# The last block's input products one group ahead, output operands three row tiles ahead, and the next stage's weights behind the residuals

## The chip, the cores and the metric

The kernel runs on one core of a Trainium2 chip. The metric is the device time of one execution in microseconds (us). A core has five engines with queues of their own: PE (TensorE: matrix products, and transposes done as products), DVE (VectorE), ACT (ScalarE), POOL (GpSimd) and SP (SyncE, which here issues nearly all DMAs). Each engine takes its instructions in the order written; between engines they wait on semaphores.

## The reference

One inference step of a small hybrid decoder: a recurrent layer (Hawk/Griffin RG-LRU), then a layer of forgetting attention. It runs on a prompt of 2048 new tokens and on 8 sequences of 8 new tokens each, which have 4096 tokens behind them in a paged cache. The width is 1024, 16 heads of 64. All is in float32.

```python
def recurrent_mixer(x, h0, conv_buf, w_in, conv_w, conv_b, w_ga, b_ga, w_gx, b_gx, lam, w_out):
    z = x @ w_in
    u, g = z[..., :D_RNN], z[..., D_RNN:]
    u, new_buf = causal_conv(u, conv_buf, conv_w, conv_b)
    h, h_last = rg_lru(u, h0, w_ga, b_ga, w_gx, b_gx, lam)
    return (h * jax.nn.silu(g)) @ w_out, h_last, new_buf

# in rg_lru, over 8 blocks of 128 columns:
    r = sigmoid(ub @ w_ga + b_ga); i = sigmoid(ub @ w_gx + b_gx)
    log_a = -RGLRU_C * r * softplus(-lam); a = exp(log_a)
    h[t] = a * h[t-1] + sqrt(-expm1(2 * log_a)) * (i * u)

# in run_group: layer 0 is recurrent, then the shared keys and values, then attention
x = x + rms_norm(recurrent_mixer(rms_norm(x, a_pre_norm), ...), a_post_norm)
k, v, logf = shared_kv(x, kv_norm, w_kv, b_f)
x = x + rms_norm(fox_mixer(rms_norm(x, b_pre_norm), k, v, ...), b_post_norm)
```

The outputs are both x, the new keys, values and log forget values, and the recurrent and convolution states.

## The kernel before

The tokens are worked in two chunks. Chunk 0 has the 64 sample tokens (all 8 sequences) and 1024 prompt tokens, chunk 1 the rest. A float32 product is made of three products of rounded parts (`mm3`): high by high (L367), low by high (L368), high by low (L369). So a float32 operand exists as two tiles, such as `uh` and `ul`.

**Recurrence** (`phase_a1`). For each of 8 column blocks (`KB` = 8, index `n`), the chunk's tokens come in three groups (320, 384 and 384 columns in chunk 0; 384, 384 and 256 in chunk 1). For a group, PE makes the u columns (24 matmuls), ACT copies them out of PSUM (`up`), DVE does the convolution (`uc`), POOL rounds it to `uh`, DVE makes the rest `ul`. Then come the gate products (6 matmuls, `gate`) on `uh` and `ul`, and PE makes the g columns (24 matmuls). The gates of one group are issued after the u product of the next one, ahead of its g product (`pend`, `gated`). ACT turns gates into decay, DVE scans the recurrence, POOL multiplies by the gated g (`tg`), and the result, as `oh` and `ol`, is written to DRAM by SP (L641, L642).

**Output** (`phase_a2`). For each row tile of up to 128 tokens, SP loads the transposed operands `ohT` and `olT` back (L757) and the residual rows `xt` (L759). PE makes the product with w_out in two halves of 512 columns (`y`, 24 matmuls each) in the order (0,0), (1,0), (0,1), (1,1), (2,0), (2,1) and so on, first the tile and then the half. PSUM has four buffers of the kind that y uses. After the second half `post` takes sums of squares on ACT, a reciprocal root on DVE, `x` from y (L777), which frees y, and adds the residual on POOL. `finish` transposes the normed rows for the next stage. `ohT` and `olT` have two buffers each, and the load of tile i + 2 is issued when tile i is done. The pieces of w_out come in `wst` buffers (L466) and are split into `woh` and `wol` by ACT and DVE while the last block runs.

**Keys, values, queries** (`phase_b`) takes its weights through `Feed` (L399): `fetch` issues loads, `take` gives out split weights. The first two fetches are made when the stage is set up, and where they land on SP's queue is the scheduler's choice. **Decode** for the cached sequences runs in 16 turns. Two of them stand beside chunk 0's `phase_b`, the rest beside chunk 1's and beside the attention of the prompt.

The program is written once in an order of emission, and a scheduler with a model of durations then places the instructions of every engine. So an edit at one place can move others. `later` puts a piece off by some steps; `tc.issue_after(instruction)` keeps what is inside it behind an instruction.

SP's queue is strict: a DMA whose operands are not ready holds up all behind it.

Of the kernel before, what the change touches and what calls it, by code (L numbers as in the profile page):

```python
# [11 lines left out]
F32 = mybir.dt.float32  # L12
# [72 lines left out]
def tile_hawk_fox(  # L85
# [481 lines left out]
    def phase_a1(s, xs, a0, covered, feed, wk, out, then, begin):  # L567
# [82 lines left out]
        def decayed(tr, ti):  # L650
# [7 lines left out]
            elif len(ready) == len(s.groups):  # L658
# [2 lines left out]
                scans.extend(ready)  # L661
                ready.clear()

        for n in range(KB):
            W = feed.take()
            gst = wk.tile([P, 2, P], F32, name="gst", tag="gst")
            S.dma_start(gst[:, 0, :], a_w_ga[0, n])
            S.dma_start(gst[:, 1, :], a_w_gx[0, n])
            gh = wk.tile([P, 2, P], F32R, name="gh", tag="gh", bufs=2)
            gl = wk.tile([P, 2, P], F32R, name="gl", tag="gl", bufs=2)  # L670
            cp(G, gh[:, :, :], gst[:, :, :])
            tt(G, gl[:, :, :], gst[:, :, :], f(gh[:, :, :]), ALU.subtract)
            for gi, (c0, C) in enumerate(s.groups):
                while covered < c0 + C:
                    covered = next(a0)
                so = sm if c0 == 0 else 0
                tn = C - so
                xh, xl = xs[gi]
                rh, rl = (lambda k: xh[:, k, :]), (lambda k: xl[:, k, :])
                up = wk.tile([P, 3 + mh], F32, name="up", tag="up", bufs=2)  # L680
                cp(G, up[:, 0:3], halo[:, n, :])
                ups = mmp("u")
                mm3(ups[:, :C], W.h(0, P), W.l(0, P), rh, rl, KB)
                us = None
                if so:
                    us = wk.tile([P, DB, 3 + DS], F32, name="us", tag="us")
                    cp(G, us[:, :, 0:3], gv[:, n, 11:35].rearrange("p (b j) -> p b j", b=DB))
                    A.copy(us[:, :, 3:], ups[:, :sm].rearrange("p (b q) -> p b q", b=DB))
                A.copy(up[:, 3:3 + tn], ups[:, so:C])
                uc, uh, ul = front(n, c0, C, ups, us, up, W)  # L690
                if so and n == 0:
                    decays()
                if pend:
                    trti = gated()
                gps = mmp("g")
                mm3(gps[:, :C], W.h(P, 2 * P), W.l(P, 2 * P), rh, rl, KB)
                if pend:
                    decayed(*trti)
                tg = wk.tile([P, mh], F32, name="tg", tag="tg", bufs=5)
                A.activation(tg[:, :C], gps[:, :C], AF.Tanh, scale=0.5)  # L700
                V.scalar_tensor_tensor(tg[:, :C], tg[:, :C], 1.0, gps[:, :C], op0=ALU.add, op1=ALU.mult)
                if scans:
                    scan(*scans.pop(0))
                pend = (n, c0, C, uc, uh, ul, tg, gh, gl)
# [19 lines left out]
    def states(s, pool):  # L724

        for st, cnt, done in ((st_s, 32, s.i == 0), (st_p, 4, s is sca[-1])):
            if not done:
                continue
            for j in range(2):
# [9 lines left out]
                else:  # L739
                    S.dma_start(conv_p[0, 0][:, sl], so[0:3, :])  # L740
                    S.dma_start(rnn_p[0][:, sl], so[3:4, :])

    def phase_a2(s, out, pool, put):

        lds, yps = {}, {}

        def load(i):
            if i >= len(s.tiles):
                return
            col, m, samp, tok = s.tiles[i]  # L750
            oh = pool.tile([P, KB, P], F32R, name="ohT", tag="ohT", bufs=2)
            ol = pool.tile([P, KB, P], F32R, name="olT", tag="olT", bufs=2)
            c0 = max(lo for lo, _ in s.groups if lo <= col)

            for lo, hi in ((0, 4), (4, KB)) if i < 2 else ((0, KB),):
                for t, d in ((oh, s.oh[c0]), (ol, s.ol[c0])):
                    S.dma_start(f(t[:, lo:hi, :m]), d[lo * P:hi * P, col - c0:col - c0 + m].rearrange("(k p) t -> p k t", p=P))  # L757
            xt = pool.tile([P, D], F32, name="xt", tag="xt", bufs=4)
            S.dma_start(xt[:m, :], xs_flat if samp else xp_flat[tok:tok + m])  # L759
            lds[i] = oh, ol, xt  # L760

        def product(i, j):
            col, m, samp, tok = s.tiles[i]
# [1077 lines left out]
```

## Time and profile before

| | us |
|---|---|
| runs shown | 3066.45, 3070.52, 3083.66 (median 3070.52) |
| profiled execution, its own time | 3073.57 |
| its span | 3071.8 |
| PE busy in the span | 2826.8 (92%) |
| chunk 0: last u and g products, then y from | 241.5 to 275.9, then 278.7 |
| chunk 1: last block from, y from, tile 2 from | 1077.8, 1104.3, 1137.7 |

The profile is one execution, taken by the hardware. Its timelines give the start and the length of an instruction, and in brackets how long its engine had been idle before it and what ended that. The ends of matmuls are modelled: a row's length overlaps the next one, so that the pace of matmuls is read from one start to the next. A window's row gives the busy time of each engine, then the clock granted to PE as a share of full speed (PEclk), the mean busy share of the DMA engines, and GB/s. The DMA engines are busy for 0.88 or more of every 100 us from 1200 to 2500, when the cache is read for decode.

### The profile page before, as it was taken

The numbers are of one execution on the slowest core, as the hardware profiler recorded it, in microseconds if no ns is written. First come the engines' busy times: TensorE is split into PE (matmuls) and PEld (weight loads), VectorE is DVE, ScalarE is ACT, GpSimd is POOL, SyncE is SP. The second block draws the span as 40 slices with busy tenths as digits, with TensorE's granted clock in tenths as the row PEclk, the third lists the DMA queues.
The fourth block names the chain that finished last, engine by engine and source line by source line (L and its number), as shares of the span: only waits on it lengthen the run. The fifth ranks groups of instructions, "written<-read, shape, count | busy, mean of one in ns | idle before, by whom it ended". The sixth has DMA issues, their size and how long they took to land.

```text
span 3071.8 us, 58144 instructions
## 1 busy us (share of the span) xinstructions
PE 2826.8 (92%) x20462; PEld 2178.9 (71%) x20462; DVE 1805.2 (59%) x4012; ACT 1294.9 (42%) x2874; POOL 1158.7 (38%) x1263
## 2 busy tenths in 40 slices
PE   5998999999999989997999798998989989999898
PEld 5997889988999978896888454555545554554587
DVE  7876555424357756755555566666667765543244
ACT  4665432222346655333333244343434445455321
POOL 1653201000025532000000365656565757788522
PEclk9999999999999999998999799999999999999999
DMA  4224547788622256999999998989999997322243
GB/s 121 91 76 147 157 137 209 239 256 260 209 82 86 86 180 202 318 312 313 329 311 316 303 285 258 293 276 306 294 309 316 328 286 236 107 67 68 83 143 111
DMA packets 492855, 653.25 MB, mean 213 GB/s; under 512 B 91100, under 2 KB 292829, under 8 KB 485286
## 3 DMA queue, kind: packets, MB, share of 16 engines
q1 hardware_dynamic: 488934, 643.87, 66.8%
q10 hardware_dynamic: 3340, 3.56, 0.4%
q8 instruction: 162, 2.65, 0.4%
q0 software_dynamic: 288, 2.10, 0.2%
q14 instruction: 131, 1.07, 0.1%
HBM read 513.82 MB, written 135.16 MB: 211 GB/s over the span
## 4 chain that ended last, share of the span: by engine, by line
PE 56%; DMA 18%; DVE 10%; ACT 6%; SPq 5%; issue 4%; POOL 2%; DVEq 0%; ACTq 0%; POOLq 0%
PE ops L1558 6%; DMA raw<-in_cache_k_dram 4%; PE y L367 4%; PE y L368 4%; PE y L369 4%; PE st L1538 4%; DMA raw<-in_cache_v_dram 4%; PE sx L1405 3%; PE kv L369 3%; PE kv L367 3%; PE kv L368 3%; PE dO L1236 3%; PE st L1539 3%; PE dS L1126 2%; PE qg L367 2%
## 5 line engine op out<-in xcount | busy, mean ns | idle before, releaser
L105 POOL TENSOR_TENSOR acc<-acc,p 128x512 f32<-128x512 f32 (+3 forms) x576 | 640.6, 1112 | 304.6 <-PE ops L1558 240.8
L1547 ACT ACTIVATE p<-st 128x512 f32<-128x512 f32 (+3 forms) x576 | 290.5, 525 | 409.5 <-PE st L1539 186.6
L1158 DVE STREAM_TRANSPOSE ktr<-raw 128x1024 f32<-128x1024 f32 x256 | 305.3, 1224 | 151.2 <-DMA raw<-in_cache_k_dram 141.8
L1407 DVE TENSOR_REDUCE mxs<-sx 128x1 f32<-128x512 f32 x384 | 253.6, 679 | 145.0 <-PE sx L1405 144.2
L368 PE MATMUL kv<-wl,xh 128*128 128x256 f32 (+3 forms) x1088 | 309.9, 288 | 9.0 <-DVE wl L412 8.8
L367 PE MATMUL kv<-wh,xh 128*128 128x256 f32 (+3 forms) x1088 | 311.0, 290 | 5.8 <-ACT wh L411 5.7
L369 PE MATMUL kv<-wh,xl 128*128 128x256 f32 (+3 forms) x1088 | 310.1, 287 | 0.0
L1558 PE MATMUL ops<-p,vvt 128*64 128x512 f32 (+3 forms) x1152 | 296.9, 554 | 2.3 <-ACT p L1547 2.1
L1538 PE MATMUL st<-qa,ka 128*128 128x512 f32 (+3 forms) x640 | 273.6, 428 | 21.1 <-ACT p L1547 16.6
L1405 PE MATMUL sx<-kbt,qbt 96*128 96x512 f32 (+3 forms) x640 | 232.3, 421 | 26.3 <-DMA qbt<-qd 10.6
L1538 PEld LDWEIGHTS st<-qa,ka 128*128 128x128 f32 x640 | 124.1, 194 | 179.5 <-issue 112.9
L411 ACT ACTIVATE wh<-wst,gv 128x256 fp32r<-128x256 f32 (+1 forms) x384 | 164.4, 499 | 187.7 <-DMA wst<-in_b_w_in_dram 73.2
L1539 PE MATMUL st<-qbt,kbt 128*128 128x512 f32 (+3 forms) x640 | 236.5, 371 | 0.0
L412 DVE SCALAR_TENSOR_TENSOR wl<-wst,gv,wh 128x256 fp32r<-128x256 f32 (+1 forms) x384 | 170.4, 494 | 104.6 <-ACT wh L411 100.8
L367 PE MATMUL qg<-xh,wh 128*128 128x384 f32 (+2 forms) x640 | 228.8, 359 | 0.0
L369 PE MATMUL qg<-xh,wl 128*128 128x384 f32 (+2 forms) x640 | 227.6, 357 | 1.1 <-DVE wl L412 1.0
L368 PE MATMUL qg<-xl,wh 128*128 128x512 f32 (+2 forms) x640 | 227.0, 356 | 0.0
L1091 POOL TENSOR_TENSOR qw<-qb,amask 128x128 f32<-128x128 f32 x64 | 29.8, 473 | 502.7 <-PE dS L1126 354.0
L368 PEld LDWEIGHTS kv<-wl,xh 128*128 128x128 f32 (+1 forms) x1088 | 204.3, 189 | 12.7 <-DVE wl L412 10.4
L367 PEld LDWEIGHTS kv<-wh,xh 128*128 128x128 f32 (+1 forms) x1088 | 204.3, 189 | 12.2 <-ACT wh L411 6.5
L369 PEld LDWEIGHTS kv<-wh,xl 128*128 128x128 f32 (+1 forms) x1088 | 206.0, 190 | 4.4 <-issue 4.3
L1405 PEld LDWEIGHTS sx<-kbt,qbt 96*128 96x128 f32 x640 | 117.6, 201 | 93.7 <-issue 31.1
(299 smaller groups left out, 6477.2 us busy)
## 6 DMA issues: line engine op xcount, KB each, us to landing
raw<-in_cache_k_dram SPq DMA_DIRECT2D x512, 256.0 KB
raw<-in_cache_v_dram SPq DMA_DIRECT2D x512, 256.0 KB
wst<-in_w_kv_dram SPq DMA_DIRECT2D x48, 512.0 KB
wst<-in_b_w_in_dram SPq DMA_DIRECT2D x48, 512.0 KB
xt<-in_x_prompt_dram SPq DMA_DIRECT2D x32, 512.0 KB
wst<-in_a_w_in_dram SPq DMA_DIRECT2D x64, 256.0 KB
out_dram<-kf SPq DMA_DIRECT2D x128, 128.0 KB
sc<-cd SPq DMA_DIRECT2D x16, 1024.0 KB
```

The costliest lines, as they stand in the source:

```text
L105: eng.tensor_tensor(out, a, b, op=op)
L367: T.matmul(ps, lh(k), rh(k), start=(k == 0), stop=False)
L368: T.matmul(ps, lh(k), rl(k), start=False, stop=False)
L369: T.matmul(ps, ll(k), rh(k), start=False, stop=(k == nk - 1))
L412: V.scalar_tensor_tensor(wl[:, k, :], st[:, k, :], gk, f(wh[:, k, :]), op0=ALU.mult, op1=ALU.subtract)
L1158: V.transpose(t.kts[pp][:, n], raw[:, :, pp * 256:(pp + 1) * 256])
L1405: T.matmul(ps[:, :w], qb[0:96, j * P:(j + 1) * P], kb[0:96, ck * 512:ck * 512 + w], start=True, stop=True)
L1407: V.reduce_max(mx[:, j, ck:ck + 1], ps[:, :w], axis=AX.X)
L1538: T.matmul(ps[:, lo:], ka[:, ks], qa[:, lo:], start=True, stop=False)
L1539: T.matmul(ps[:, lo:], kb[:, ks], qb[:, lo:], start=False, stop=(k < qc * 4))
L1547: pair.append((k, lo, p, A.activation(p[:, lo:], ps[:, lo:], AF.Exp)))
L1558: return T.matmul(ops[r:r + HD, lo:], vvs[h % 2][:, k, :], p[:, lo:], start=(k < 2), stop=(last and k >= todo[-1][0] - 1))
```

## The change

Three things. First, in the last block alone, the u product of the next group is made ahead of this group's g product (the loop body is cut into `columns`, which makes u, and `gelu`, which makes g). PE's order of products in that block was u0, gates of the block before, g0, u1, gates 0, g1, u2, gates 1, g2. It is now u0, gates of the block before, u1, g0, gates 0, u2, g1, gates 1, g2, then gates 2. Second, `ohT` and `olT` have `deep` buffers, two in chunk 0 as before and three in chunk 1 (`2 + s.i`); the load of a tile is parted from that of its residual. Third, the first two fetches of the next stage's weights are kept behind the fifth residual load of the chunk.

```diff
-            for gi, (c0, C) in enumerate(s.groups):
...
+            made, ng = [], len(s.groups)
+            for gi in range(ng):
+                if len(made) == gi:
+                    made.append(columns(n, gi, W))
+                trti = gated() if pend else None
+                if n == KB - 1 and gi + 1 < ng:
+                    made.append(columns(n, gi + 1, W))
+                gelu(n, gi, W, gh, gl, trti, *made[gi])
                 if n == KB - 1:
                     if gi == 0:
                         out.fetch()
...
+    rows_in = []
+
     def phase_a2(s, out, pool, put):
 
-        lds, yps = {}, {}
+        lds, yps, deep = {}, {}, 2 + s.i
+        rows_in.clear()
...
-            oh = pool.tile([P, KB, P], F32R, name="ohT", tag="ohT", bufs=2)
-            ol = pool.tile([P, KB, P], F32R, name="olT", tag="olT", bufs=2)
+            oh = pool.tile([P, KB, P], F32R, name="ohT", tag="ohT", bufs=deep)
+            ol = pool.tile([P, KB, P], F32R, name="olT", tag="olT", bufs=deep)
...
-            for lo, hi in ((0, 4), (4, KB)) if i < 2 else ((0, KB),):
+            for lo, hi in ((0, 4), (4, KB)) if i < deep else ((0, KB),):
...
+        def residual(i):
...
             xt = pool.tile([P, D], F32, name="xt", tag="xt", bufs=4)
-            S.dma_start(xt[:m, :], xs_flat if samp else xp_flat[tok:tok + m])
-            lds[i] = oh, ol, xt
+            rows_in.append(S.dma_start(xt[:m, :], xs_flat if samp else xp_flat[tok:tok + m]).ins)
+            lds[i] += (xt,)
...
-        load(0)
-        load(1)
+        for i in range(2):
+            load(i)
+            residual(i)
         apostB = pool.tile([P, D], F32, name="apostB")
         S.dma_start(apostB[:, :], a_post_norm.broadcast_to([P, D]))
+        if deep > 2:
+            load(2)
...
                 post(i)
-                load(i + 2)
+                load(i + deep)
+                residual(i + 2)
...
-            feed.fetch()
-            feed.fetch()
+            with tc.issue_after(rows_in[4]):
+                feed.fetch()
+                feed.fetch()
```

The lines move with it: the operand loads are L776, the residual L784, x from y L802, the store of x L804, the copy of u L682, tanh of g L698.

The scheduler's order changes with these edits. PE at the end of tile 1 in chunk 1, with buffer numbers; before, `y_12502` is tile 0's second half, `y_12581` tile 1's:

```order
L369 MATMUL y_12502<-woh7_12473,olT_12357 128x512
L367 MATMUL y_12502<-woh7_12473,ohT_12356 128x512
L368 MATMUL y_12502<-wol7_12474,ohT_12356 128x512
L369 MATMUL y_12502<-woh7_12473,olT_12357 128x512
L368 MATMUL y_12581<-wol5_12464,ohT_12364 128x512
L369 MATMUL y_12581<-woh5_12463,olT_12365 128x512
L367 MATMUL y_12581<-woh5_12463,ohT_12364 128x512
L368 MATMUL y_12581<-wol5_12464,ohT_12364 128x512
L369 MATMUL y_12581<-woh5_12463,olT_12365 128x512
L367 MATMUL y_12581<-woh6_12469,ohT_12364 128x512
L368 MATMUL y_12581<-wol6_12470,ohT_12364 128x512
```

Ten more of `y_12581` follow there, then two transposes of states (`stp`) and tile 2. Of the changed kernel, where the three are `y_12508`, `y_12587` and, for tile 2, `y_12666`:

```order
L369 MATMUL y_12508<-woh7_12479,olT_12357 128x512
L367 MATMUL y_12508<-woh7_12479,ohT_12356 128x512
L368 MATMUL y_12508<-wol7_12480,ohT_12356 128x512
L369 MATMUL y_12508<-woh7_12479,olT_12357 128x512
L368 MATMUL y_12587<-wol7_12480,ohT_12364 128x512
L369 MATMUL y_12587<-woh7_12479,olT_12365 128x512
L367 MATMUL y_12587<-woh7_12479,ohT_12364 128x512
L368 MATMUL y_12587<-wol7_12480,ohT_12364 128x512
L369 MATMUL y_12587<-woh7_12479,olT_12365 128x512
L367 MATMUL y_12666<-wh_12267,ohT_12374 128x512
```

Tile 0's last matmul stood 17 matmuls ahead of tile 1's end; now it stands 5 ahead. In chunk 0 it was 13 and is 5.

SP at the first loads of the output stage in chunk 1. `oh_0`, `oh_384` and `oh_768` are the DRAM arrays of the three groups; L641 and L642 write them and the loads read them. Before:

```order
L757 DMA ohT<-oh_0_63 128x4x128
L757 DMA olT<-ol_0_66 128x4x128
L759 DMA xt<-in_x_prompt_dram 128x1024
L757 DMA ohT<-oh_0_63 128x4x128
L757 DMA olT<-ol_0_66 128x4x128
L759 DMA xt<-in_x_prompt_dram 128x1024
L802 DMA apostB<-in_a_post_norm_dram 128x1024
L759 DMA xt<-in_x_prompt_dram 128x1024 x2
L641 DMA oh_0_63<-oh 128x384
L642 DMA ol_0_66<-ol 128x384
```

With the change:

```order
L641 DMA oh_768_65<-oh 128x256
L642 DMA ol_768_68<-ol 128x256
L641 DMA oh_0_63<-oh 128x384
L642 DMA ol_0_66<-ol 128x384
L776 DMA ohT<-oh_0_63 128x4x128
L776 DMA olT<-ol_0_66 128x4x128
L776 DMA ohT<-oh_0_63 128x4x128
L776 DMA olT<-ol_0_66 128x4x128
L784 DMA xt<-in_x_prompt_dram 128x1024
L776 DMA ohT<-oh_0_63 128x4x128
```

The first halves (rows 0 to 3 of 8) stood ahead of the stores of blocks 6 and 7. Now they stand behind the first group's stores of block 7 and directly ahead of the second halves. In chunk 0 a load of w_out (`wst`), which stood directly ahead of the first operand load, is now behind the loads of tiles 0 and 1.

SP at tile 2 in chunk 1, before:

```order
L641 DMA oh_384_64<-oh 128x384
L642 DMA ol_384_67<-ol 128x384
L641 DMA oh_768_65<-oh 128x256
L642 DMA ol_768_68<-ol 128x256
L399 DMA wst<-in_w_kv_dram 128x4x256
L399 DMA wst<-in_w_kv_dram 128x4x16
L399 DMA wst<-in_w_kv_dram 128x4x256
L399 DMA wst<-in_w_kv_dram 128x4x16
L399 DMA wst<-in_b_w_in_dram 128x4x256
L757 DMA ohT<-oh_0_63 128x8x128
L757 DMA olT<-ol_0_66 128x8x128
```

With the change:

```order
L804 DMA x_76<-x_12533 128x1024
L776 DMA ohT<-oh_384_64 128x8x128
L776 DMA olT<-ol_384_67 128x8x128
L784 DMA xt<-in_x_prompt_dram 128x1024
L399 DMA wst<-in_w_kv_dram 128x4x256
L399 DMA wst<-in_w_kv_dram 128x4x16
L804 DMA x_76<-x_12612 128x1024
L399 DMA wst<-in_w_kv_dram 128x4x256
L399 DMA wst<-in_w_kv_dram 128x4x16
L399 DMA wst<-in_b_w_in_dram 128x4x256
L776 DMA ohT<-oh_768_65 128x8x128
L776 DMA olT<-ol_768_68 128x8x128
```

The loads of the next stage's weights (L399) stood ahead of tile 2's operands. Now they are behind the fifth residual, and tile 2's operands are issued with those of tiles 0 and 1, further up. The loads `ohT<-oh_768` are later tiles.

Further on, attention rows and decode turns are laid out differently: ahead of the sum of the last decode turn PE's order had 1,850 of the 2,816 rows of attention (`st`, `sx` and `ops`), and has 1,800 with the change.

More of the change, by code (lines that the diff above doesn't have):

```diff
@@ L662, in decayed, with columns, gelu @@
                 ready.clear()
+        def columns(n, gi, W):
+            nonlocal covered
+            c0, C = s.groups[gi]
+            while covered < c0 + C:
+                covered = next(a0)
+            so = sm if c0 == 0 else 0
+            tn = C - so
+            xh, xl = xs[gi]
+            up = wk.tile([P, 3 + mh], F32, name="up", tag="up", bufs=2)
+            cp(G, up[:, 0:3], halo[:, n, :])
+            ups = mmp("u")
+            mm3(ups[:, :C], W.h(0, P), W.l(0, P), lambda k: xh[:, k, :], lambda k: xl[:, k, :], KB)
+            us = None
+            if so:
+                us = wk.tile([P, DB, 3 + DS], F32, name="us", tag="us")
+                cp(G, us[:, :, 0:3], gv[:, n, 11:35].rearrange("p (b j) -> p b j", b=DB))
+                A.copy(us[:, :, 3:], ups[:, :sm].rearrange("p (b q) -> p b q", b=DB))
+            A.copy(up[:, 3:3 + tn], ups[:, so:C])
+            made = front(n, c0, C, ups, us, up, W)
+            if so and n == 0:
+                decays()
+            return made
+        def gelu(n, gi, W, gh, gl, trti, uc, uh, ul):
+            nonlocal pend
+            c0, C = s.groups[gi]
+            xh, xl = xs[gi]
+            gps = mmp("g")
+            mm3(gps[:, :C], W.h(P, 2 * P), W.l(P, 2 * P), lambda k: xh[:, k, :], lambda k: xl[:, k, :], KB)
+            if trti:
+                decayed(*trti)
+            tg = wk.tile([P, mh], F32, name="tg", tag="tg", bufs=5)
+            A.activation(tg[:, :C], gps[:, :C], AF.Tanh, scale=0.5)
+            V.scalar_tensor_tensor(tg[:, :C], tg[:, :C], 1.0, gps[:, :C], op0=ALU.add, op1=ALU.mult)
+            if scans:
+                scan(*scans.pop(0))
+            pend = (n, c0, C, uc, uh, ul, tg, gh, gl)
         for n in range(KB):
@@ L672, in phase_a1 @@
             tt(G, gl[:, :, :], gst[:, :, :], f(gh[:, :, :]), ALU.subtract)
-            for gi, (c0, C) in enumerate(s.groups):
[L674 to L704, printed above, removed]
+            made, ng = [], len(s.groups)
[6 more added lines that the diff above has]
+                gelu(n, gi, W, gh, gl, trti, *made[gi])
                 if n == KB - 1:
```

4 lines of the change are left out of this document (added).

## The prediction

> **What bounds the kernel now.** I read the page first, then the waits of TensorE (PE) in the two stretches that the change touches, then their timelines. The page's busy times and its attention groups (line, operation, count, busy time, mean):
>
> ```profile
> PE 2826.8 (92%) x20462; PEld 2178.9 (71%) x20462; DVE 1805.2 (59%) x4012; ACT 1294.9 (42%) x2874; POOL 1158.7 (38%) x1263
> ...
> L1558 PE MATMUL ops<-p,vvt 128*64 128x512 f32 (+3 forms) x1152 | 296.9, 554 | 2.3 <-ACT p L1547 2.1
> L1538 PE MATMUL st<-qa,ka 128*128 128x512 f32 (+3 forms) x640 | 273.6, 428 | 21.1 <-ACT p L1547 16.6
> L1405 PE MATMUL sx<-kbt,qbt 96*128 96x512 f32 (+3 forms) x640 | 232.3, 421 | 26.3 <-DMA qbt<-qd 10.6
> L1539 PE MATMUL st<-qbt,kbt 128*128 128x512 f32 (+3 forms) x640 | 236.5, 371 | 0.0
> ```
>
> PE is busy for 92%, so in most places only its idle time can be won: 245 us in all (3071.8 less 2826.8). The change reaches a small part of it. PE's waits up to 420 us (chunk 0), then from 860 to 1260 us (chunk 1); columns are the time in total, the times, the longest:
>
> ```profile
> PE gate L367 <- POOL uh L100: 11.7, 8, 2.7
> ...
> PE gate L367 <- POOL uh L100: 8.0, 6, 3.9
> PE y L367 <- DMA ohT<-oh: 7.1, 2, 6.0
> ```
>
> Most of the gate time belongs to earlier blocks, which stay as they are. PE's timeline at the end of chunk 0's recurrence (start, length, what, and in brackets the idle time before it):
>
> ```profile
> 249.56 0.34 PE L367 MATMUL u<-xh,wh 128*128 128x384 f32 x1
> ...
> 253.75 0.31 PE L367 MATMUL gate<-uh,gh 128*128 128x320 f32 x1
> ...
> 266.17 0.61 PE L367 MATMUL gate<-uh,gh 128*128 128x384 f32 x2 [1.71 <-POOL uh L100]
> 268.57 0.44 PE L368 MATMUL gate<-ul,gh 128*128 128x384 f32 x1 [0.92 <-DVE ul L105]
> ...
> 274.34 0.62 PE L367 MATMUL gate<-uh,gh 128*128 128x384 f32 x2 [2.71 <-POOL uh L100]
> ...
> 278.73 0.69 PE L367 MATMUL y<-wh,ohT 128*64 128x512 f32 x1 [2.82 <-DMA ohT<-oh]
> ...
> 305.28 0.47 PE L367 MATMUL y<-wh,ohT 128*128 128x512 f32 x1 [1.08 <-DVE x L777]
> ...
> 307.00 0.50 PE L369 MATMUL y<-wh,olT 128*128 128x512 f32 x1 [1.00 <-DMA olT<-ol]
> ```
>
> So here PE loses 5.34 us to gates, 2.82 to the first operand load, 2.08 at tile 2. The same place in chunk 1:
>
> ```profile
> 1099.89 0.44 PE L367 MATMUL gate<-uh,gh 128*128 128x384 f32 x1 [0.51 <-POOL uh L100]
> ...
> 1104.28 0.39 PE L367 MATMUL y<-wh,ohT 128*128 128x512 f32 x1
> ...
> 1108.48 0.39 PE L367 MATMUL y<-wh,ohT 128*128 128x512 f32 x1
> 1108.71 0.40 PE L367 MATMUL gate<-uh,gh 128*128 128x256 f32 x2
> ...
> 1111.87 0.47 PE L367 MATMUL y<-wh,ohT 128*128 128x512 f32 x1 [1.12 <-DMA ohT<-oh]
> ...
> 1137.70 0.76 PE L367 MATMUL y<-wh,ohT 128*128 128x512 f32 x1 [6.01 <-DMA ohT<-oh]
> ```
>
> The wait of 6.01 us at tile 2 is the largest that the change aims at, and SyncE's queue tells why it is there:
>
> ```profile
> 1127.33 2.12 SPq L399 DMA_DIRECT2D wst<-in_w_kv_dram  x4
> 1129.49 0.50 SPq L399 DMA_DIRECT2D wst<-in_b_w_in_dram  x1
> 1130.10 0.88 SPq L757 DMA_DIRECT2D ohT<-oh  x1
> ```
>
> Five weight loads stand ahead of tile 2's operands, and those are issued 7.6 us before PE uses them (1130.10 to 1137.70).
>
> **Part 1, the u product a group ahead.** No instruction is added. One u product of 384 columns takes 4.19 us (249.56 to 253.75); with one more between a group's columns and its gates, its conv and POOL's uh get that much more time. The three waits in chunk 0 are at most 2.71, so I take all 5.34 us away, and 0.51 in chunk 1. What is late next is the load of ohT. SP's rows before and behind y's start in chunk 0:
>
> ```profile
> 271.10 0.32 SPq L641 DMA_DIRECT2D oh<-oh  x1
> ...
> 273.94 0.38 SPq L466 DMA_DIRECT2D wst<-in_a_w_out_dram  x1
> 274.42 0.42 SPq L757 DMA_DIRECT2D ohT<-oh  x1
> ...
> 301.04 0.39 SPq L757 DMA_DIRECT2D ohT<-oh  x1
> ```
>
> ohT takes memory that the last g product still reads. That product ended before the idle time of 2.71 us, at 271.6; without 1.71 and 0.92 it ends at 269.0. The w_out load of 273.94 is now behind. From issue to use took 4.3 us (274.42 to 278.73), so y starts at about 273.3: 5.4 us earlier. That needs the oh store of 271.10, ahead of it on SP, to come at 268 or 269; ScalarE's square root now precedes one oh copy that stood ahead of it, which gives those 2 to 3 us. If the store stays at 271.10, y starts near 276 and 2.7 is left.
>
> At tile 2 of chunk 0 there are still two operand buffers: its load (301.04) waits for the last use of tile 0. In the listed order 13 matmuls of tile 1 stood behind that, now 5. At 0.233 us each (18 from 1104.28 to 1108.48 took 4.20) the wait grows by 8 x 0.233 = 1.9. Chunk 0: 5.4 - 1.9 = 3.5 us gained; bounds 0.8 (the late store) and 7 (the listed order costs nothing, and 1.5 of clock, below, comes back).
>
> **Part 2, three operand buffers in chunk 1.** The first half of tile 0's load no longer has an old buffer: by its listed place it goes behind the oh stores of block 7, and it waits for the last g product. Before, y began at 1104.28 with no wait. Now the g product ends 0.51 earlier, at 1103.8, the gates fill 0.7 (1108.71 to the next y), and the load needs 3.1 to 4.3 us from issue: the shorter from the second halves, issued at 1108.73 and used at 1111.87, the longer from chunk 0. Y starts at 1106.9 to 1108.1; I take 1107.2. Then 96 matmuls at 0.233 are 22.4 us, and some small transposes: tile 1 ends at 1130.3, against 1131.7 (1137.70 less 6.01).
>
> Tile 2's four loads are issued as soon as SP reaches them, so 6.01 goes. In its place comes the PSUM slot: y has four buffers, and tile 2 needs the one that tile 0's norm frees.
>
> ```profile
> 1108.73 0.92 SPq L757 DMA_DIRECT2D ohT<-oh  x2
> ...
> 1127.06 0.60 ACT L498 ACTIVATE junk<-y 128x512 bf16<-128x512 f32 x1 [0.63 <-PE y L369]
> ...
> 1130.26 1.41 DVE L777 SCALAR_TENSOR_TENSOR x<-y,nr_y,apostB 128x512 f32<-128x512 f32 x2
> ```
>
> From the sum of squares (1127.06) to the first x (half of 1.41 behind 1130.26) are 3.9 us. Behind tile 0's last matmul stood 17 of tile 1, now 5, which are 1.2 us: a new wait of 2.7. Tile 2 starts at 1133.0, 4.7 earlier than 1137.70.
>
> **The clock.** Waits have a tail here. Windows in chunk 0, then chunk 1 (PEclk is the third value from the end):
>
> ```profile
> 308.00:312.00 4.00, 4.00 (x13) 3.14 (x12) 1.70 (x14) 2.82 (x8) 0.27 (x1) 0.62 0.80 197
> ...
> 1138.00:1142.00 4.00, 4.00 (x10) 2.99 (x10) 0.00 (x0) 0.00 (x0) 0.00 (x0) 0.50 1.16 317
> 1142.00:1146.00 4.00, 4.00 (x15) 3.11 (x15) 3.19 (x22) 0.35 (x1) 0.00 (x0) 0.77 0.18 66
> ```
>
> After 6.01 us idle the clock was 0.50 and 0.77: 4 x 0.50 + 4 x 0.23 = 2.9 us lost. After two waits of 1.08 and 1.00 it was 0.62 in one window: 4 x 0.38 = 1.5. A new wait of 2.7 I price as the smaller loss, so 1.4 comes back at tile 2; the new wait at y's start can cost 1.5. Together nothing to plus 1.4. Chunk 1: 4.7 + 0.3 = 5.0; bounds 1 (the first load takes two microseconds longer and the clock drops twice) and 8 (no new wait at tile 2).
>
> The Trainium skill, "TensorE: Matmul & The Clock Gate", section "What's actually happening", says that the clock is halved after an idle window of about 3.4 us that runs freely. By that rule the two new waits, each under 3.4, should cost nothing, and the gain would be about 1.5 us larger. The trace speaks against reading it so: the 308 to 312 window is slow behind two waits that are 2.1 together.
>
> **Part 3, weights behind the residuals.** The fifth residual, on SP, and the first copies of these weights, on ScalarE:
>
> ```profile
> 1152.72 1.26 SPq L759 DMA_DIRECT2D xt<-in_x_prompt_dram  x1
> ...
> 1201.84 1.77 ACT L411 ACTIVATE wh<-wst,gv 128x272 fp32r<-128x272 f32 x4 [0.66 <-PE y L369]
> ```
>
> The five loads of 1127.33 move behind the former. The copies wait for nothing but the last y product, so 49 us of y products (1152.72 to 1201.84) hide the loads and their 2.6 us of issue: cost nothing. Without that cover it would be one load time, about as long as ohT's 4.3.
>
> **Part 4, what nobody asked for.** The planner has laid attention and decode differently. Ahead of the last decode turn's sum the listed order had 1,850 of 2,816 attention rows; now 1,800. The attention groups quoted above are 1,039 us; 50/2816 of that is 18.4 us of PE work that no longer covers decode loads. Whether it is missed depends on the loads; windows of 100 us, then a wait of PE from 2000 us on:
>
> ```profile
> 2300.00:2400.00 100.00, 95.25 (x923) 56.92 (x922) 74.00 (x155) 44.52 (x111) 58.34 (x59) 0.98 1.00 316
> 2400.00:2500.00 100.00, 96.72 (x825) 53.97 (x825) 69.56 (x145) 47.48 (x114) 69.22 (x65) 0.98 1.00 325
> ...
> PE dO L1236 <- DMA raw<-in_cache_v_dram: 16.6, 12, 5.1
> ```
>
> The DMA share is 1.00, so the loads set the pace at least in part; PE's idle time is under 5% there, so much of the cover is slack. Cost between 0 and 18.4. The value nearest to a row is a quarter: PE's 8.0 us idle in those 200 (200 less 95.25 and 96.72) is 4%, so most late loads are met by other work. I take 4.
>
> **Sum.** -3.5 - 5.0 + 4 = -4.5 us on the profiled execution, which took 3073.6: 3069. The median of the runs is 3070.5, three below it; the same change there gives 3066, which I predict.
>
> **Rivals.**
> *A. The waits only change place.* The late oh store keeps chunk 0 at 0.8, chunk 1 keeps 1, and part 4 eats it: -1.8 + 4, so 3069 to 3073. For it: each stage has three waits in a row within 30 us. Against: the 6.01 had a plain cause that is gone.
> *B. Full gain.* Chunk 0 gives 7, chunk 1 gives 8, decode costs nothing: -15, 3055.5. For it: PE is over 95% busy at 2300. Against: both chunks would have to lose no time on PSUM slots.
> *C. Slower: decode is paced by its loads.* Place: the turns from about 2000 to 2560. If the cache loads alone set the end of the last turn, it ends 8.5 us earlier, as the stages before do, but 18.4 us of attention is left over behind it: +10, 3080.5. It decides when the loads are back to back over the whole stretch; DMA share 1.00 speaks for it, PE's 95% against. Were the earlier start lost as well, 3089.
> *D. The change does nothing in chunk 0*, since two buffers stay there and the wait comes back at tile 2: -5 + 4, 3072.6.
>
> **Chances.** Forecast 0.40, D 0.07, A 0.17, B 0.20, C 0.16. The likeliest one's own range is 3059 to 3070; that of 8 in 10 takes in B's and C's centres: 3053 to 3083. A measurement here can tell about 0.5% (15 us): faster by that (under 3055.2) is most of B and what lies beyond, 0.22; slower (over 3085.9) is C with the start lost, and shifts that no row shows, 0.12; the rest 0.66.
>
> **What would show it.** Right: no gate wait over 1 us in the last block; y of chunk 0 starting near 273 with one ohT wait of about 3; in chunk 1 a first ohT wait of about 3, at tile 2 a wait of about 3 for DVE's x in place of 6.01 for ohT, and PEclk over 0.6 behind it. The decode end at about 2555 with attention left. Wrong: an oh store still near 271; a wait for woh or wol in chunk 1 above 1 us, since w_out's last load is now behind an oh store on SP; dO's waits for cache loads from 2000 on grown by more than 8 us; weights late at 1205.

## The result, and the profile after

The changed kernel took 3094.3 us (median of 8 runs, 3091.45 to 3104.24) against 3073.6 for the kernel before in the same runs: the ratio is 1.0072, 95% interval 1.0055 to 1.0089. It is slower by about 21 us, outside the range on record, and on the other side of the forecast. Its profiled execution, the fastest of the eight, took 3091.45 us with a span of 3089.7, which is 17.9 over the span before. TensorE (PE) is busy nearly as long as before (2830.3 against 2826.8 us), so most of the loss is idle time: 259.4 us of the span against 245.0.

The ends of the recurrence first. PE's waits in the two stretches of the changed kernel, up to 420 us and from 860 to 1260 us (time in total, times, longest):

```profile
PE gate L367 <- POOL uh L100: 8.1, 7, 1.9
PE y L367 <- DMA ohT<-oh: 4.6, 2, 3.2
PE tps L508 <- DVE xl L105: 4.0, 5, 1.9
...
PE gate L367 <- POOL uh L100: 7.1, 5, 3.4
PE tps L508 <- DVE xl L105: 3.7, 3, 1.8
PE y L367 <- DVE x L802: 3.0, 1, 3.0
PE y L367 <- DMA ohT<-oh: 2.6, 1, 2.6
PE gate L367 <- ACT ti L603: 1.5, 1, 1.5
PE gate L367 <- ACT tr L603: 0.9, 1, 0.9
```

In chunk 1 the 6.01 us wait for `ohT` is gone, and `x` (L802) has taken its place with 3.0, as forecast at 2.7. Two waits for ScalarE's `tr` and `ti` are new. Of the gate waits for `uh` in chunk 0 one over 1 us stays in the last block. PE's timeline of the changed kernel, chunk 0 and then chunk 1:

```profile
273.02 0.62 PE L367 MATMUL gate<-uh,gh 128*128 128x384 f32 x2 [1.55 <-POOL uh L100]
276.19 0.69 PE L367 MATMUL y<-wh,ohT 128*64 128x512 f32 x1 [1.39 <-DMA ohT<-oh]
...
305.02 0.47 PE L367 MATMUL y<-wh,ohT 128*128 128x512 f32 x1 [3.20 <-DMA ohT<-oh]
306.72 0.79 PE L369 MATMUL y<-wh,olT 128*128 128x512 f32 x1 [0.99 <-DMA olT<-ol]
...
1096.97 0.35 PE L367 MATMUL gate<-uh,gh 128*128 128x256 f32 x1 [0.86 <-ACT tr L603]
1099.23 0.58 PE L367 MATMUL gate<-uh,gh 128*128 128x256 f32 x1 [1.53 <-ACT ti L603]
1102.88 0.80 PE L367 MATMUL y<-wh,ohT 128*128 128x512 f32 x1 [2.64 <-DMA ohT<-oh]
...
1132.59 0.67 PE L367 MATMUL y<-wh,ohT 128*128 128x512 f32 x1 [2.98 <-DVE x L802]
```

To compare stages, take the time from the start of the last block's first u product to the first product of the keys and values. In chunk 0 it was 153.9 us and is 151.2. In chunk 1 it was 134.4 and is 135.2. So the ends of the recurrence gained 2.7 and lost 0.8, and the changed kernel came to chunk 1's `kv` at 1205.8 us, where the kernel before came at 1212.2. Hardly any of these 6.4 us was won by the edits there: at chunk 0's first `kv` the two kernels are 0.2 us apart (395.2 and 395.4), and chunk 1's last block already starts 7.1 us earlier (1070.6 for 1077.8). That start lies between 1067.2 and 1078.6 in the fourteen kernels of this case, and what sets it is not shown.

The loss comes later. The last decode product (`dO`) of the kernel before, then of the changed one, each with the row of a window from 1250 to 2500 us (PE busy is the second value, the last three are PEclk, the DMA share and GB/s):

```profile
2573.61 0.63 PE L1244 MATMUL dO<-rawn,dpc 128*32 128x256 f32 x4
1250.00:2500.00 1250.00, 1148.40 (x10214) 779.57 (x10215) 809.49 (x1625) 497.62 (x1235) 505.49 (x510) 0.94 0.96 306
```

```profile
2574.52 0.60 PE L1273 MATMUL dO<-rawn,dpc 128*32 128x256 f32 x4
1250.00:2500.00 1250.00, 1124.99 (x10099) 763.87 (x10098) 794.41 (x1592) 483.95 (x1204) 484.03 (x490) 0.94 0.96 304
```

Decode ends at the same time, although it was reached 6.4 us earlier and has 50 fewer rows of attention to share PE with. DMA share and rate are nearly the same. In the same 1250 us PE was busy 23.4 us less. What was not done there stands behind the decode. The rows from chunk 1's first `kv` to the end of the last `dO` and from there to the end of the span, before and then after:

```profile
1212.18:2574.24 1362.06, 1252.84 (x10982) 848.42 (x10980) 876.24 (x1810) 549.46 (x1353) 556.10 (x566) 0.95 0.95 302
2574.24:3071.80 497.56, 457.85 (x1970) 288.64 (x1970) 215.87 (x567) 199.81 (x422) 288.15 (x247) 0.97 0.35 104
```

```profile
1205.84:2575.12 1369.28, 1237.91 (x10913) 841.75 (x10911) 862.59 (x1786) 541.38 (x1337) 535.72 (x551) 0.94 0.95 300
2575.12:3089.70 514.58, 473.37 (x2040) 296.76 (x2039) 229.93 (x591) 206.95 (x438) 307.03 (x263) 0.97 0.35 102
```

PE's busy time in the two stretches together is the same (1710.7 and 1711.3 us). Behind the decode there are 70 matmuls more, the stretch is 17.0 us longer, and PE's idle time in it hardly differs (39.7 and 41.2). Ahead of the decode's end the idle time has grown, from 109.2 to 131.4. VectorE, which makes `ktr` from the cache pages (`raw`), waits longer for their loads there (window 1250 to 2560, before and then after):

```profile
DVE ktr L1158 <- DMA raw<-in_cache_k_dram: 111.2, 52, 6.5
```

```profile
DVE ktr L1187 <- DMA raw<-in_cache_k_dram: 157.5, 68, 6.8
```

This wait goes with the loss in the kernels of the same order, but it does not measure it: a kernel below that lost nearly as much waited 100.7.

### The profile page after: what moved, and what is told of

The parts are those of the page before. It is cut to its first block, busy times and chain, and to the rows that moved or that the text cites. A ratio compares the mean times of both kernels' runs of the same rounds, so it can differ in the third digit from the quotient of the medians.

```text
span 3089.7 us, 58163 instructions
## 1 busy us (share of the span) xinstructions
PE 2830.3 (92%) x20462; PEld 2185.6 (71%) x20462; DVE 1811.6 (59%) x4012; ACT 1294.3 (42%) x2874; POOL 1154.3 (37%) x1263
## 4 chain that ended last, share of the span: by engine, by line
PE 47%; DMA 18%; DVE 7%; SPq 4%; ACT 4%; issue 3%; POOL 2%; ACTq 0%; DVEq 0%; POOLq 0%
PE ops L1587 6%; DMA raw<-in_cache_k_dram 4%; DMA raw<-in_cache_v_dram 4%; PE st L1567 3%; PE kv L367 3%; PE kv L369 3%; PE kv L368 3%; PE y L367 3%; PE y L368 3%; PE y L369 3%; PE dO L1265 3%; DMA sc<-cd 3%; PE sx L1434 3%; SPq L1102 2%; PE st L1568 2%
## 5 line engine op out<-in xcount | busy, mean ns | idle before, releaser
L1434 PE MATMUL sx<-kbt,qbt 96*128 96x512 f32 (+3 forms) x640 | 237.5, 432 | 34.1 <-DMA qbt<-qd 12.9
```

Of the source, the lines that this page charges most:

```text
L1434: T.matmul(ps[:, :w], qb[0:96, j * P:(j + 1) * P], kb[0:96, ck * 512:ck * 512 + w], start=True, stop=True)
```

## The experiments

In the expectations, theory 1 says that the laying of attention against decode makes the loss, theory 2 that the edits at the ends of the recurrence do, theory 3 that the weights' place does, and theory 4 that PE's own work paces decode. "Rows ahead" is the count of attention rows in PE's listed order ahead of the last decode turn's sum: 1,850 before, 1,800 in the changed kernel. `SHARE` is a constant of the planner that says how much decode is laid beside how much other work.

### One edit at a time

**weights_only** keeps the recurrence as before and puts only the two fetches behind the fifth residual:

```diff
-            feed.fetch()
-            feed.fetch()
+            with tc.issue_after(rows_in[4]):
+                feed.fetch()
+                feed.fetch()
```

> Only the third edit: the next stage's weights behind the fifth residual. The recurrence and its output stage keep the operand loads and products of the kernel before, yet the scheduler lays attention and decode exactly as in the changed kernel: 1,800 of 2,816 attention rows ahead of the last decode turn's sum, where the kernel before has 1,850. Theory 1 (the laying of attention against decode makes the loss): the decode turns end within 5 us of before, some 18 us of attention is left behind them, and the time is 12 to 24 us over before. Theory 2 (the new products and loads at the ends of the recurrence make it, by starting the later stages at another moment): within 5 us of before, or a few us under it at tile 2 of chunk 1, where the 6.01 us wait goes.

Measured: 3091.3 us against 3070.6, ratio 1.0059 (1.0042 to 1.0076). The end of chunk 1 gained: its stretch is 127.9 us, and PE's wait for tile 2 nearly went, without a third buffer. PE's timeline there:

```profile
1128.94 0.47 PE L367 MATMUL y<-wh,ohT 128*128 128x512 f32 x1 [0.51 <-DMA ohT<-oh]
1130.65 0.50 PE L369 MATMUL y<-wh,olT 128*128 128x512 f32 x1 [1.01 <-DMA olT<-ol]
```

Its kv products begin at 1201.9, ten us ahead of before, and the last `dO` still ends within 2 us of before, with nearly as many waits for the cache as in the changed kernel:

```profile
2572.20 0.60 PE L1273 MATMUL dO<-rawn,dpc 128*32 128x256 f32 x4
...
DVE ktr L1187 <- DMA raw<-in_cache_k_dram: 153.6, 67, 7.8
```

From the first kv product to the end of that `dO`, and from there to the end:

```profile
1201.89:2572.80 1370.91, 1244.44 (x10913) 848.28 (x10911) 861.00 (x1786) 541.22 (x1337) 535.91 (x551) 0.94 0.95 299
2572.80:3094.90 522.10, 479.20 (x2040) 298.33 (x2039) 229.43 (x591) 206.76 (x438) 307.38 (x263) 0.96 0.34 101
```

Again 2,040 matmuls are left behind the decode. In this execution PE is also busy longer, by 12.9 us over the two stretches, for as many matmuls as before within one, at a granted clock of 0.94 and 0.96 where it was 0.95 and 0.97. So here a part of the longer time is the clock.

So theory 2 falls: the loss is there without the two edits that touch products and operand loads.

**u_ahead_only** is the first edit alone (`deep` 2, fetches as before):

```diff
-        lds, yps, deep = {}, {}, 2 + s.i
+        lds, yps, deep = {}, {}, 2
...
-            with tc.issue_after(rows_in[4]):
-                feed.fetch()
-                feed.fetch()
+            feed.fetch()
+            feed.fetch()
```

(against the changed kernel)

> Only the first edit: the u product a group ahead in the last block; two operand buffers and the weights where they were. Order of attention: 1,837 rows ahead of the last sum, 13 fewer than before, which by theory 1 is 13/2816 x 1,039 = 5 us of attention left behind. Theory 1: the recurrence gains what chunk 0 showed with the full change (about 3 us) and the total is within -4 to +8 us of before. Theory 2, with this edit as the cause: +15 to +20.

Measured: 3071.7 us, ratio 0.9997 (0.9984 to 1.0010). Chunk 0's stretch is 150.8 us (3.1 gained), chunk 1's 130.5 (3.9). The waits for `tr` and `ti` are here too:

```profile
1095.91 0.34 PE L367 MATMUL gate<-uh,gh 128*128 128x384 f32 x1
...
1100.80 0.36 PE L367 MATMUL gate<-uh,gh 128*128 128x256 f32 x1 [0.86 <-ACT tr L603]
1103.07 0.39 PE L367 MATMUL gate<-uh,gh 128*128 128x256 f32 x1 [1.07 <-ACT ti L603]
```

They belong to the first edit. The last group's gates start here 4.9 us behind those of the group before, where they started 8.8 behind in the kernel before (1099.89 to 1108.71), with 19 y products between. So PE now has to wait until ScalarE has read the earlier gates out of PSUM, into `tr` and `ti`.

**three_buffers_only** is the second edit alone:

```diff
-                if n == KB - 1 and gi + 1 < ng:
+                if False and gi + 1 < ng:
...
-            with tc.issue_after(rows_in[4]):
-                feed.fetch()
-                feed.fetch()
+            feed.fetch()
+            feed.fetch()
```

> Only the second edit: three operand buffers in chunk 1. Same order of attention as with the u product alone (1,837 rows). Theory 1: 0 to +10 us over before: 5 us of attention left behind, and at chunk 1 the first operand load comes late while the weights still stand ahead of nothing. Theory 2, with this edit as the cause: +15 to +20.

Measured: 3080.2 us, ratio 1.0033 (1.0021 to 1.0044), the upper edge of what theory 1 allowed. Its chunk 1 takes 135.1 us, 0.7 more than before. SyncE's row for the first operand load of chunk 1 in the kernel before, and then its rows in this kernel:

```profile
1081.15 0.46 SPq L757 DMA_DIRECT2D ohT<-oh  x1
```

```profile
1094.21 0.32 SPq L641 DMA_DIRECT2D oh<-oh  x1
...
1096.21 0.39 SPq L776 DMA_DIRECT2D ohT<-oh  x1
```

The last block starts at 1067.2 here, and at 1077.8 before, so that the load has moved from 3.4 us behind that start to 29.0 us behind it. It now comes behind the store, as the listed order had it. Y starts 32.1 us behind the block's start, where it was 26.5. At tile 2 it waits 2.97 us for `x` where it waited 6.01 for `ohT`. What the third buffer saves at tile 2 it costs at tile 0.

### Two edits, with known orders

**u_and_buffers** takes away only the weights edit. PE's, ScalarE's and GpSimd's orders are then the changed kernel's, row for row.

```diff
-            with tc.issue_after(rows_in[4]):
-                feed.fetch()
-                feed.fetch()
+            feed.fetch()
+            feed.fetch()
```

> The change without its third edit. The listed order of TensorE, ScalarE and GpSimd is row for row that of the changed kernel (1,800 attention rows ahead of the last decode sum); only the five weight loads and rows around them on SyncE stand elsewhere. Theory 1 (the laying of attention against decode sets the time): as slow as the changed kernel, +16 to +24 us over before. Theory 3 (new; the weights' place on the queue is what costs, since the run with that edit alone was the slow one): within 8 us of before.

Measured: 3098.4 us against 3074.1, ratio 1.0088 (1.0055 to 1.0121).

**u_and_weights** takes away only the three buffers. PE's order is that of the u product alone.

```diff
-        lds, yps, deep = {}, {}, 2 + s.i
+        lds, yps, deep = {}, {}, 2
```

> The change without its three buffers. TensorE's order is row for row that of the u product alone (1,837 rows), which took the time of before; the weights stand behind the fifth residual. Theory 1: -8 to +2 us against before, since the weights alone gained 6.5 us at tile 2 of chunk 1 and the order is the harmless one. Theory 3: +14 to +22, as with the weights alone.

Measured: 3069.2 us, ratio 0.9989 (0.9971 to 1.0006). The weights edit is in the faster kernel of this pair and not in the slower one, so theory 3 falls. What the change, weights_only and u_and_buffers share is the order with 1,800 rows ahead.

### The planner's constant alone

Two kernels are the kernel before with nothing but another `SHARE`:

```diff
-SHARE = 1.13
+SHARE = 1.21
```

> The kernel before with SHARE 1.21 in place of 1.13, and nothing of the change: 1,722 attention rows ahead of the last decode sum, 128 fewer. If the cache loads pace the decode turns (theory 1), the last turn ends within 12 us of before, 47 us of attention (128/2816 of 1,039) is left over behind it, and the time is +30 to +50. If TensorE's own work paces them (theory 4), the last turn ends some 47 us earlier and the total is within 8 us of before.

> The kernel before with SHARE 1.17: 1,812 rows ahead of the last sum, 38 fewer (14 us), and less attention ahead of the early turns (1,016 rows at turn 11 where before has 1,108). Theory 1: +8 to +20. Theory 4: within 6 us of before.

Measured: with 1.21, 3090.9 us, ratio 1.0056 (1.0033 to 1.0078); with 1.17, 3090.3, ratio 1.0068 (1.0043 to 1.0092), as theory 1 had it. So an order alone can cost nearly as much as the change did (16 to 17 us by the medians, for 21). The last `dO` of 1.21:

```profile
2560.96 0.60 PE L1244 MATMUL dO<-rawn,dpc 128*32 128x256 f32 x4
1250.00:2500.00 1250.00, 1122.80 (x10241) 766.97 (x10241) 799.69 (x1589) 478.93 (x1189) 474.32 (x483) 0.94 0.97 307
```

With 128 rows fewer to run beside it, decode ended 12.6 us earlier, not 47: PE's own work does not set most of its pace, and theory 4 falls. But it did end earlier, by slightly more than the 12 us allowed, so theory 1 was too high as well (17 us measured where 30 to 50 were expected): from the decode's end to the end were 532.4 us, 34.8 more than before. For 128 rows that is 0.27 us a row, where 0.37 was reckoned. And VectorE did not wait longer for the cache than in the kernel before:

```profile
DVE ktr L1158 <- DMA raw<-in_cache_k_dram: 100.7, 52, 5.7
```

### The same edits in another order

**all_share_114** is the whole change with `SHARE` 1.14, which lays 1,852 rows ahead:

```diff
-SHARE = 1.13
+SHARE = 1.14
```

> The whole change, with the planner's constant SHARE at 1.14 in place of 1.13. The ends of the recurrence are those of the changed kernel; the order of attention comes out with 1,852 of 2,816 rows ahead of the last decode sum, as many as before the change. Theory 1: the loss goes, the 6 us by which the changed kernel entered the decode stretch earlier stays in part: -8 to +4 us against before. Theory 2: still +14 to +22. In between would say that the place of the turns within the stretch matters beside the count at its end.

Measured: 3087.3 us, ratio 1.0063 (1.0045 to 1.0081): a miss for the count. By its time alone it lies where theory 2 had it; all_share_1128 below speaks against that reading. In its profiled execution decode ends late, at 2579.5, and 502.1 us stand behind it. Enough attention was ahead, and decode itself was slower in this execution: from the sum of turn 2 to that of turn 15 it took 1214.4 us, where the kernel before took 1205.0 and the changed one 1204.2. In two further kernels with the changed one's order these turns took 1200.6 (u_and_buffers) and 1205.9 (weights_only), so executions of one order of PE lie 5 us apart in it. That the place of the rows along the turns matters too would fit the rest; it is not shown.

Four more ask whether the last count can be trusted when the turns before are alike. The edits are of that one constant, on the kernels named:

```diff
-SHARE = 1.13
+SHARE = 1.1275
```

(weights_only)

> The weights edit alone, as in weights_only, with SHARE 1.1275 in place of 1.13: the only aim is another laying of attention, with 1,837 rows ahead of the last decode sum in place of 1,800. Theory 1 (the laying makes the loss; the loads fix the decode end): the last decode product ends within 12 us of 2570, the stretch from there to the end is 495 to 505 us where weights_only had 513, and the time is -6 to +6 us against before, where weights_only was +18. Theory 3 (the weights edit itself costs): again +14 to +22.

Measured: 3067.1 us against 3074.2, ratio 0.9977 (0.9960 to 0.9994). The kernel that was 18 us slower than before (by its ratio) is 7 us faster than before. Its last `dO`, its window, and VectorE's wait:

```profile
2567.74 0.62 PE L1273 MATMUL dO<-rawn,dpc 128*32 128x256 f32 x2
1250.00:2500.00 1250.00, 1142.71 (x10240) 777.99 (x10238) 806.76 (x1615) 493.39 (x1224) 496.30 (x502) 0.94 0.96 305
...
DVE ktr L1187 <- DMA raw<-in_cache_k_dram: 110.5, 53, 8.6
```

```diff
-SHARE = 1.13
+SHARE = 1.128
```

(the whole change)

> The whole change with SHARE 1.128: 1,837 rows ahead of the last decode sum in place of 1,800. Theory 1: most of the loss goes, 0 to +12 us against before, where the change was +22; what stays is the 2 to 7 us that three buffers cost at the end of chunk 1. If the count were only a token of something else in the change: +18 or more.

Measured: 3070.9 us, ratio 0.9994 (0.9975 to 1.0012). All three edits are in it, and the loss is not: its median lies 3 us under before, where 0 to +12 was expected.

```diff
-SHARE = 1.13
+SHARE = 1.125
```

(u_and_weights)

> The u product ahead and the weights edit, which together took -5 us against before, now with SHARE 1.125: the counts of attention rows are near the same up to turn 13 and then fall to 1,795 at the last. Theory 1: 42 rows or 15 us less attention ahead of the decode end, which stays within 10 us of 2561: +4 to +14 us against before. If the laying did not matter: -5 again.

Measured: 3083.3 us, ratio 1.0030 (1.0013 to 1.0048). With 42 rows fewer ahead, the two edits go from 5 us under before (with an interval that includes no change) to 9 us over it, inside what was expected; decode ends at 2566.0, five later.

```diff
-SHARE = 1.13
+SHARE = 1.10
```

(u_and_weights)

> The same two edits with SHARE 1.10: 1,836 rows ahead of the last sum, but more ahead of the early turns (1,312 at turn 12 where the kernel with 1.13 has 1,279). By the count at the end: -8 to +2 us. The run of the whole change at SHARE 1.14 had 1,852 rows and was slow, with its decode end late; if more attention ahead of the early turns makes the decode end late, +6 to +16 here.

Measured: 3079.7 us, ratio 1.0019 (1.0003 to 1.0035). At 5.5 us over before it lies between the two expectations. Its turns 2 to 15 took 1212.8 us where u_and_weights took 1208.4, which is within what one order varies by, and its decode ends 7 us later, at 2568.0. So it is not shown that more attention ahead of the early turns slows them. And 515.2 us stand behind that, more than other kernels have with this count. The rows from the last `dO` to the end, of u_and_weights and then of this kernel:

```profile
2560.92:3068.20 507.28, 466.60 (x2012) 291.30 (x2011) 219.20 (x574) 203.17 (x430) 300.93 (x259) 0.98 0.34 101
```

```profile
2568.03:3083.20 515.17, 473.65 (x2016) 295.45 (x2014) 221.49 (x579) 204.12 (x434) 300.47 (x258) 0.96 0.34 100
```

PE has four matmuls more and is busy 7.1 us longer, which is most of the 7.9: nearly the same work at a granted clock of 0.96 in place of 0.98. Why the clock was lower there is open.

All fourteen kernels, from one profiled execution each (us from the start of the span; the ratio is that of the runs, which is not the quotient of the medians given above and differs from it by up to 0.0015). Executions of one kernel lie up to 22 us apart, and a profiled one can lie some us from the median: that of all_share_1128 took 3078.7 us for a median of 3070.9, that of three_buffers_only 3075.8 for 3080.2.

| kernel | rows ahead | chunk 1's stretch | end of the last dO | from there to the end | ratio |
|---|---|---|---|---|---|
| before | 1,850 | 134.4 | 2574.2 | 497.6 | 1 |
| weights_share_11275 | 1,837 | 126.5 | 2568.4 | 500.3 | 0.9977 |
| u_and_weights | 1,837 | 129.0 | 2560.9 | 507.3 | 0.9989 |
| all_share_1128 | 1,837 | 135.2 | 2576.2 | 500.7 | 0.9994 |
| u_ahead_only | 1,837 | 130.5 | 2560.1 | 510.7 | 0.9997 |
| u_weights_share_110 | 1,836 | 133.3 | 2568.0 | 515.2 | 1.0019 |
| u_weights_share_1125 | 1,795 | 129.3 | 2566.0 | 517.6 | 1.0030 |
| three_buffers_only | 1,837 | 135.1 | 2564.7 | 509.4 | 1.0033 |
| before_share_121 | 1,722 | 132.2 | 2561.6 | 532.4 | 1.0056 |
| weights_only | 1,800 | 127.9 | 2572.8 | 522.1 | 1.0059 |
| all_share_114 | 1,852 | 135.1 | 2579.5 | 502.1 | 1.0063 |
| before_share_117 | 1,812 | 131.7 | 2566.8 | 518.3 | 1.0068 |
| the change | 1,800 | 135.2 | 2575.1 | 514.6 | 1.0072 |
| u_and_buffers | 1,800 | 135.6 | 2574.8 | 521.6 | 1.0088 |

The last `dO` ends between 2560 and 2580 in every one of them, while the stretch behind it spans 497 to 532. No kernel with 1,812 rows ahead or fewer was as fast as before. But three_buffers_only and all_share_114, with more rows, were slower than before too, so the count alone does not decide. It is also taken at the last sum and not at the last `dO`: of the five kernels with 1,837 rows, the two with about 500 us behind the decode have 1,992 and 1,993 matmuls left there, the three with 507 to 511 have 2,011 or 2,012. Chunk 1's stretch is 134.4, 131.7 and 132.2 in three kernels that have the same code there, so a difference below 3 us in that column says little.

## Why the prediction was wrong, point by point

**The step that failed is part 4.** It took a quarter of 18.4 us, 4, as the price of the 50 rows of attention, because PE was idle for only 4% of the 200 us from 2300 on. The quarter follows from no row: 4% of 18.4 would be 0.7, and a quarter is 4.6. Little idle time can mean that the loads have slack, or that attention covers the waiting for them; the runs fit the second. What the runs showed in place of 4 is 17.0 us behind the decode's end, which came no earlier: 2575.1 for 2574.2. A row that pointed there was quoted beside it, a DMA share of 1.00. If the loads, at 0.96 of all DMA time over 1250 us, set when decode ends, both follow; that they do is inferred. Rival C named this mechanism and its place, with a price of 18.4 us less an earlier end of decode, and added that 3089 would follow "were the earlier start lost as well": the profiled execution took 3091. It was given 0.16. One sign that the prediction named for being wrong did not come: `dO`'s waits for cache loads from 2000 us on went from 16.6 us to 13.2.

That an earlier start was lost is the second half of it. The sum carried the gains of chunks 0 and 1 to the end, as if a stage that ends earlier moved all behind it. The changed kernel was 6.4 us ahead at 1206 us, however it came by them, and 0.9 behind at 2575.

**Part 1** held in its gain, in part by luck. In this trace the last block of chunk 0 starts 2.6 us later than before. Less that, the oh store of 271.74 came at 269.1 (268 or 269 was needed) and y began at 273.6, where 273.3 was forecast. But of the 5.34 us of gate waits 1.74 stayed (1.55 for `uh`, 0.19 for `ul`), the operand load was issued at 271.1 where the working had 269.0, and from issue to use it took 2.45 us, not 4.3. The two errors about the load cancel. Tile 2 then waited 4.2 us (3.20 and 0.99) against 2.08, which is 2.1 more; 1.9 was forecast. Chunk 0 gained 2.7 us, and 3.1 with the first edit alone, for 3.5. Not foreseen were the gates' waits for `tr` and `ti` in chunk 1, 0.86 and 1.53 us.

**Part 2** was wrong in sign: chunk 1 was to gain 5.0 and lost 0.8 (within what equal code varies by). The wait for x at tile 2 came as forecast, 2.98 for 2.7. But y began 32.2 us behind the block's start, where the working gave 29.4 (1107.2 less 1077.8), by the waits for `tr` and `ti`; and the clock was charged too little. The windows of the changed kernel around the start of y, cut where the clock changes:

```profile
1095.20:1098.61 3.41, 1.63 (x11) 1.18 (x9) 1.92 (x3) 2.04 (x5) 2.06 (x4) 1.00 0.00 0
1098.61:1102.02 3.41, 1.01 (x3) 0.71 (x3) 2.32 (x4) 3.41 (x7) 0.00 (x0) 0.50 0.63 181
1102.02:1105.43 3.41, 2.56 (x6) 1.88 (x7) 3.15 (x5) 3.39 (x6) 0.00 (x0) 0.50 1.06 299
1105.43:1108.85 3.42, 3.42 (x9) 2.54 (x9) 1.31 (x2) 3.35 (x5) 1.19 (x3) 0.50 1.11 325
1108.85:1112.26 3.41, 3.41 (x19) 2.69 (x18) 2.16 (x4) 2.58 (x6) 1.72 (x3) 1.00 1.10 367
```

The clock fell to 0.50 at 1098.61, within the second of the three waits (0.86, 1.53 and 2.64), and stayed there until 1108.85. From y's start at 1102.88 half of these 5.97 us is lost, 3.0 us, where the working had 1.5 at most. The Trainium skill, "TensorE: Matmul & The Clock Gate", section "What's actually happening", ties the half clock to an idle window of about 3.4 us. No single wait here is that long, and in the 3.41 us ahead of the fall PE was busy for 1.63. Read as one gap, the rule doesn't fit these rows; read as the share of a window it may, but what share it takes is not measured here.

**Part 3** held as far as it went: PE's waits up to 1260 us list none for the moved weights. The cost came by way of the order, which part 3 did not price: 18 us in weights_only. Nor does the weights edit alone take the 6.01 us away. Each of the three edits does: at tile 2 PE then waits 0.51 and 1.01 us in weights_only, 1.61 and 0.83 in u_ahead_only, 2.97 in three_buffers_only, while 5.7 stay in the two kernels with only another constant. Weights alone shortened chunk 1's stretch by 6.5 us (and by 7.9 in the other order), while all three edits together lengthened it by 0.8.

**Rival A**, waits that change place, is what happened at the ends of the recurrence in chunk 1. **Rival D** put the gain of chunk 0 at nothing; it kept 2.7. (Its 3072.6 is reckoned from the profiled execution; from the median, as for rivals B and C, it would be 3069.5.) **Rival B** needed both chunks to lose no time on PSUM slots, and chunk 1 lost 2.98 on one.

What is shown: the order with fewer attention rows ahead is enough to make the loss (weights_only, the kernel before with another constant), and another order is enough to remove it with all three edits in place (all_share_1128). What is only inferred is the pace set by the loads: no run had fewer of them. Which part of an order counts, beside the rows ahead of the last sum, stays open, and so does the part of the granted clock: PE's busy time from chunk 1's `kv` on is the same in the kernel before and in the changed one, but not in weights_only.

## What to carry to other kernels

Where a scheduler lays two streams of work beside each other, compare its whole order before trusting a local sum: an edit of five DMAs took 50 rows of attention from ahead of the decode's end, over a thousand us further on, and that outweighed everything the edit was for. Here, beside a stream of loads with a DMA share of 0.96, a lead of 6.4 us was not carried to the end, and rows of other work that left the stream's shadow were paid at 0.27 to 0.34 us of their 0.37. If local gains of a few us are the aim, hold the order fixed, or try a few values of the planner's constant with each edit: here 1.1275 in place of 1.13 turned an edit from 18 us slower than before into 7 us faster.

## What had not been expected of the hardware

The clock halved behind waits that were each short, as above: it fell to 0.50 behind 3.41 us in which PE was busy for 1.63, with the wait of 0.86 us and the first part of the one of 1.53 in them, and stayed there for 10.2 us. And the load stream hardly minds what PE does: over 1250 us its rate was 303 to 307 GB/s at a share of 0.95 to 0.97 in all fourteen kernels, while PE's busy time in that window went from 1122.8 to 1148.4 us.
